# Two transformer blocks on one core: the attention's merge moved by two tiles, output weights placed elsewhere, the expert choice of block 2 cut in three

## The chip, the cores and the metric

The kernel runs on one core of a Trainium2 chip. A core has five engines with instruction queues of their own: TensorE (PE, matmuls and transposes), VectorE (DVE), ScalarE (ACT), GpSimd (POOL) and SyncE (SP, which here only issues DMAs). An engine takes its instructions strictly in order; it waits for others by semaphores. The metric is the device time of one execution in microseconds; lower is better.

## What is computed

1024 tokens of width 1024 go through two blocks in float32. Block 1 has an RG-LRU branch and a multi-head attention branch, which are gated and summed, an output projection, and 32 experts. Block 2 has a hybrid mixer (gated linear attention and pooling), an output projection with layer norm, and 64 experts. The parts that matter here, shortened:

```python
# block 1, 16 heads of 64: chunk-causal attention, then the merge with the other branch
yb = mla(q_c, kv_c, k_pe, ...)          # softmax(q k^T) v, per head
merged = gates[:, :, 0] * ya + gates[:, :, 1] * yb
h = h + merged @ w_out
# block 2
p = multiscale_pool(u, w_pool, pool_scale)
mix = concatenate([o, p], axis=-1)
h = layer_norm(ALPHA * h + mix @ w_out_2, ln1_g, ln1_b)
# expert choice: 4 of 8 groups by the sum of their two best, then 8 of the experts left
scores = sigmoid(h @ w_router); sel = scores + router_bias
gidx  = top_k(top_k(sel by groups of 8, 2).sum(-1), 4)
eidx  = top_k(sel where the group is chosen, 8)
wts   = scores[eidx] / sum * 2.5
```

## The kernel before

Matmuls that need float32 accuracy are made of three float32r matmuls: each operand is split into a high part (ACT, a copy that rounds) and a low part (DVE, the operand minus the high part); `split` (L247, L253), `split_ps` (L259 to L263) and `mm3` (L271 to L273) do this.

**Attention** (`attention`, L834). Heads run one after the other; a head has eight key tiles `kt` of 128. For each tile PE makes the scores `st` (L947 to L949), ACT their exponential `raw` (L950), and three tiles later PE multiplies by the values (L958). `st` has three PSUM buffers, so a scores matmul waits when ACT is three exponentials behind. Beside the tiles, `beside(h, kt)` puts the work for the next head into `fill`: transposes of q and k in tiles 0 and 1 (PE L901, ACT L259 and L262, DVE L260 and L263), row maxima in tiles 3 to 6 (PE L916 into `tm`, three PSUM buffers, DVE L919 and L921), the last reduction `row_piece` after tile 7 (DVE L925, then PE L929). After tile 6 and in tile 2 of the next head `finish` copies the head's output to `y` (ACT L971) and sends its row sums off (SP L973); in tile 4 of the next head `rec` inverts them (DVE L980), writes them to memory (SP L981) and reads them back spread over partitions into the tile `rec` (SP L984), of which there is one.

Heads 2p and 2p+1 are merged as pair p, in six parts of `merge`: part 0 (POOL L992) in the even head 2p+2; parts 1 to 5 in the odd head 2p+3: part 1 (DVE L992) and part 2 (DVE L994) in tile 0, part 3 (DVE L996) in tile 1, part 4 (ACT L999, the high part `mgh`, two of 128x512) and part 5 (DVE L1002, the low part `mgl`, two of 128x512). Part 5 ends with `gates(pr + 1)`: two loads of 512 KB on SP (L1013) for the next pair. `MERGE` (L832) names for each part the first head and the tile. Head 15 has no next head and fewer pieces.

**Mixer of block 2** (`mixer2`, L2048). Its tiles come from pools; `hc` (`c1`, bufs 1, with `v`), `hw` (`wp`, weights, bufs 2), `hs` (`slot()`, ten of 128x1024) are opened in this order and lie so in memory. At its end (L2333 on) the pool weights `wpl` are loaded and split, `v` is transposed back (PE L2353, L263 on DVE writes `mxl`), and four `pool(g)` run.

**Output projection of block 2** (`mixer_out2`, L2366). It loads the output weights in eight pieces of 512 KB (SP L2388) into three tiles `s0`, `s1`, `s2`, and splits each (ACT L247 `woh`, DVE L253 `wol`). These tiles lie over places that the mixer used, so a load waits until the last reader of what lay there is done. Then ten rounds t: for t below 8, 96 matmuls in two halves with DVE L2461 after each, then `norm(t)`: DVE L2407 to L2410, ACT L291 (square root), DVE L292 to L2412, ACT L2414, DVE L2415 (times g), POOL L2416 (plus b; on DVE for t = 7). In round t the half 0 ends with `trans(t-2)` (PE L2428, ACT L2429), the half 1 with `router(t-2)` (PE L2435, ACT L2436 `lg`, ACT L2438 `ah`). After `router(3)` stands the whole expert choice of tokens 0 to 511, `route2` (L2466), a generator with seven pieces of DVE work; its first needs a Tanh on ACT (L2475), which changes ACT's function table, and the next square root changes it back.

Of the kernel before, what the change touches and what calls it, by code (L numbers as in the profile page):

```python
# [7 lines left out]
F32 = mybir.dt.float32  # L8
F32R = mybir.dt.float32r
# [222 lines left out]
class Body:  # L232
# [596 lines left out]
            while posts:  # L829
                step()  # L830

    MERGE = (2, 0), (3, 0), (3, 0), (3, 1), (3, 1), (3, 2)  # L832

    def attention(self, rb, rk, ml):  # L834

# [2 lines left out]
        nc, tc, IN = self.nc, self.tc, self.IN  # L838
        with ExitStack() as cx:
# [227 lines left out]
            def beside(h, kt):  # L1067

                n = h + 1
                fill = []  # L1070
                if kt == 0 and h % 2:
                    load(h // 2 + 2)
                if n < 16:
                    if kt < 2:
                        fill += [(t_piece, n, "kq"[kt], half) for half in range(2)]
                    fill += [(m_piece, n, i, a) for i, a in
                             {3: [(7, 0), (7, 512), (6, 0)], 4: [(6, 512), (5, 0), (5, 512)],
                              5: [(4, 0), (4, 512), (3, 0)], 6: [(2, 0), (1, 0), (0, 0)]}.get(kt, ())]
                    if kt == 5:
                        fill.append((v_piece, n))  # L1080
                    if kt == 7:
                        fill += [(lambda: None,), (row_piece, n)]
                if kt == (3 if h == 15 else 4) and h > 0:
                    fill.append((rec, h - 1))
                if h == 15 and kt == 6:
                    fill.append((merge, 7, 0, 0, 2, nc.vector))
                for part, (late, at) in enumerate(self.MERGE):
                    if h >= late and (h - late) % 2 == 0 and kt == at:
                        fill.append((merge, (h - late) // 2, part, 0, 2, nc.vector if part else nc.gpsimd))
                return fill  # L1090

            self.wo, self.W = {}, {}
# [955 lines left out]
    def mixer2(self, u2):  # L2048

        nc, tc, IN = self.nc, self.tc, self.IN  # L2050
        win = IN["w_in_2"][0]
        with ExitStack() as cx:
            c1 = cx.enter_context(tc.tile_pool(reuse_waits="tile", name="hc", bufs=1))
            wp = cx.enter_context(tc.tile_pool(reuse_waits="tile", name="hw", bufs=2))
            sp = cx.enter_context(tc.tile_pool(reuse_waits="tile", name="hs", bufs=10))
            ep = cx.enter_context(tc.tile_pool(reuse_waits="tile", name="he", bufs=1))
            up = u2.enter_context(tc.tile_pool(reuse_waits="tile", name="u2", bufs=1, side="right"))
# [273 lines left out]
            self.mgh = mix.tile([128, 8, S], F32R, name="mxh")  # L2331
            self.mgl = mix.tile([128, 8, S], F32R, name="mxl")
            with tc.tile_pool(reuse_waits="tile", name="hq", bufs=2, space=PSUM) as pp, tc.tile_pool(reuse_waits="tile", name="hqt", bufs=4, space=PSUM) as pt:  # L2333
                wpl = wp.tile([128, 4, 128], F32, name="w")
                nc.sync.dma_start(wpl, IN["w_pool_2"][0].rearrange("g c d -> c g d"))
                wplh = wp.tile([128, 4, 128], F32R, name="wh")
                wpll = wp.tile([128, 4, 128], F32R, name="wl")
                self.split(wpl, wplh, wpll)
                hg = c1.tile([128, 4], F32, name="hg")
                nc.vector.tensor_scalar(hg, self.v("hg_norm_g_2", 0, 4), 0.5, None, op0=OP.mult)  # L2340

                def pool(g):
                    ph, pl = PH[g]
                    ps = pp.tile([128, S], F32, name="mm")
                    for n in range(2):
                        sl = slice(n * 512, n * 512 + 512)
                        self.mm3(ps[:, sl], [(wplh[:, g], wpll[:, g], ph[:, sl], pl[:, sl])])
                    self.split_ps(ps, self.mgh[:, 4 + g], self.mgl[:, 4 + g], self.v("pool_scale_2", g))

                def back(half, k):  # L2350
                    ps = pt.tile([128, 512], F32, name="tp")
                    for i in range(4):
                        nc.tensor.transpose(ps[:, i * 128:i * 128 + 128], v[:, half * 4 + i, k * 128:k * 128 + 128],  # L2353
                                            self.ident)
                    sl = slice(half * 512, half * 512 + 512)
                    self.split_ps(ps, self.mgh[:, k, sl], self.mgl[:, k, sl], hg[:, k:k + 1])

                for half in range(2):
                    for k in range(4):
                        back(half, k)  # L2360
                        if k % 2:
                            pool(half * 2 + k // 2)
# [3 lines left out]
    def mixer_out2(self, mo):  # L2366
# [5 lines left out]
        with ExitStack() as cx:  # L2372
# [58 lines left out]
            def router(t):  # L2431
# [5 lines left out]
                ah = ep.tile([128, D], F32, name="ah", bufs=1)  # L2437
                nc.scalar.activation(self.plain(ah), self.turned(xf), AF.Copy, scale=self.ALPHA)  # L2438
                (nc.gpsimd if t > 4 else nc.sync).dma_start(self.acc_d[t * 128:t * 128 + 128], ah)
                if t == 3:  # L2440
                    for _ in self.route2(rtp, lg[0], bias, 0, 4):
                        pass
            self.route_late = lambda rp: self.route2(rp, lg[1], bias, 4, 8)
            self.pre2 = {}

# [2 lines left out]
            for t in range(10):  # L2448
# [4 lines left out]
                for half in range(2):  # L2453
                    if t < 8:
# [4 lines left out]
                                     [(self.mgh[:, k, ts_], self.mgl[:, k, ts_], h[:, k], lo[:, k]) for k in range(8)])  # L2459
                        hs = X[t][:, half * 512:half * 512 + 512]  # L2460
                        nc.vector.scalar_tensor_tensor(hs, hs, self.ALPHA, ps, op0=OP.mult, op1=OP.add)  # L2461
                    if t > 1:
                        (router if half else trans)(t - 2)
                if t < 8:
                    norm(t)
                    loadx(t + 2)  # L2466


    def route2(self, rp, lg, bias, t0, t1):
# [286 lines left out]
```

## Time and profile before

| | us |
|---|---|
| median of 3 runs (3194.46, 3202.43, 3207.52) | 3202.43 |
| profiled execution, its own time | 3195.43 |
| its span, first to last instruction | 3193.6 |
| PE busy | 2953.0 (92%) |
| DVE busy | 1814.7 (57%) |
| ACT busy | 1249.6 (39%) |
| POOL busy | 642.9 (20%) |
| granted PE clock, mean share of full speed | 0.961 |

The page's shares are means over the whole span. Which engine holds up a stage is read from that stage's own windows and from the idle time that the timeline shows in brackets ahead of an instruction, with the instruction that ended it. A granted clock of 1.00 is 2.4 GHz, 0.50 is 1.2 GHz.

### The profile page before, as it was taken

The numbers are of one execution on the slowest core, as the hardware profiler recorded it, in microseconds if no ns is written. First come the engines' busy times: TensorE is split into PE (matmuls) and PEld (weight loads), VectorE is DVE, ScalarE is ACT, GpSimd is POOL, SyncE is SP. The second block draws the span as 40 slices with busy tenths as digits, with TensorE's granted clock in tenths as the row PEclk, the third lists the DMA queues.
The fourth block names the chain that finished last, engine by engine and source line by source line (L and its number), as shares of the span: only waits on it lengthen the run. The fifth ranks groups of instructions, "written<-read, shape, count | busy, mean of one in ns | idle before, by whom it ended". The sixth has DMA issues, their size and how long they took to land. (4 is left out here: it accounts for less than half of the span.)

```text
span 3193.6 us, 41876 instructions
## 1 busy us (share of the span) xinstructions
PE 2953.0 (92%) x15865; PEld 2183.8 (68%) x15865; DVE 1814.7 (57%) x2909; ACT 1249.6 (39%) x1929; POOL 642.9 (20%) x495
## 2 busy tenths in 40 slices
PE   5999999998999996999889998978999999999995
PEld 4778778896666893655479787955666666666663
DVE  5545651666666656566446565445655555555556
ACT  3332332444445323444343324332344444444343
POOL 0000000121000103233212232112233232333320
PEclk9999999998999997999989999979999999999997
DMA  3212120244332267999720102337899999999994
GB/s 115 66 53 86 66 73 23 97 163 110 93 93 90 92 219 275 300 330 351 239 104 28 40 18 90 132 137 242 267 282 322 303 327 313 316 316 323 314 307 144
DMA packets 225885, 579.71 MB, mean 182 GB/s; under 512 B 22421, under 2 KB 104005, under 8 KB 225653
## 3 DMA queue, kind: packets, MB, share of 16 engines
q1 hardware_dynamic: 187952, 444.37, 39.6%
q0 software_dynamic: 37296, 132.55, 16.6%
q8 instruction: 127, 2.08, 0.3%
q14 instruction: 78, 0.64, 0.1%
q10 hardware_dynamic: 432, 0.06, 0.0%
HBM read 470.22 MB, written 106.64 MB: 181 GB/s over the span
## 5 line engine op out<-in xcount | busy, mean ns | idle before, releaser
L271 PE MATMUL mm<-uh,wh 128*128 128x512 f32 x640 | 252.6, 395 | 10.8 <-ACT t L505 8.8
L273 PE MATMUL mm<-uh,wl 128*128 128x512 f32 x640 | 251.8, 393 | 0.0
L272 PE MATMUL mm<-ul,wh 128*128 128x512 f32 x640 | 251.7, 393 | 0.0
L1475 PE MATMUL gups<-raw,x 128*128 128x512 f32 (+1 forms) x536 | 236.4, 592 | 0.0
L1622 ACT ACTIVATE th<-gups 128x128 f32<-128x128 f32 (+2 forms) x136 | 49.0, 361 | 418.9 <-PE gups L1475 251.0
L1691 POOL DMA_INDIRECT acc_d<-y,si x68 | 118.3, 1740 | 438.9 <-DMA acc_d<-y,si 145.9
L1623 DVE SCALAR_TENSOR_TENSOR hh<-th,gups 128x128 f32<-128x128 f32 (+2 forms) x136 | 53.1, 390 | 241.9 <-ACT th L1622 235.7
L253 DVE TENSOR_TENSOR gl<-raw,gh 128x1024 fp32r<-128x1024 f32 x142 | 168.1, 1221 | 28.4 <-ACT gh L247 28.3
L1688 DVE TENSOR_SCALAR y<-yps,wsl 128x512 f32<-128x512 f32 (+1 forms) x95 | 71.2, 750 | 196.7 <-ACT y L1686 193.8
L271 PE MATMUL gups<-gh,xh 128*128 128x512 f32 (+1 forms) x440 | 179.8, 409 | 0.9 <-ACT xh L1589 0.9
L1686 ACT ACTIVATE y<-yps,wsl 128x512 f32<-128x512 f32 (+1 forms) x100 | 68.7, 687 | 276.9 <-PE yps L1475 146.9
L273 PE MATMUL gups<-gh,xl 128*128 128x512 f32 (+1 forms) x440 | 176.4, 401 | 0.0
L272 PE MATMUL gups<-gl,xh 128*128 128x512 f32 (+1 forms) x440 | 176.1, 400 | 0.0
L1475 PEld LDWEIGHTS gups<-raw,x 128*128 128x128 f32 (+1 forms) x536 | 95.3, 183 | 116.4 <-issue 116.4
L1579 PEld LDWEIGHTS tp<-ident,xg 128*128 128x128 f32 (+2 forms) x1088 | 114.2, 144 | 74.6 <-issue 38.5
L958 PE MATMUL o<-raw,v 128*128 128x512 f32 (+3 forms) x384 | 163.4, 514 | 0.0
L271 PEld LDWEIGHTS mm<-uh,wh 128*128 128x128 f32 x640 | 121.7, 190 | 38.1 <-ACT t L505 10.6
L247 ACT ACTIVATE gh<-raw 128x1024 fp32r<-128x1024 f32 x142 | 142.9, 1054 | 10.5 <-PE gups L273 7.7
L1579 PE MATMUL tp<-ident,xg 128*128 128x128 f32 (+2 forms) x1088 | 128.5, 262 | 15.5 <-DMA xg<-xf_d,gi 7.1
L273 PEld LDWEIGHTS mm<-uh,wl 128*128 128x128 f32 x640 | 121.6, 190 | 25.7
L272 PEld LDWEIGHTS mm<-ul,wh 128*128 128x128 f32 x640 | 121.7, 190 | 25.3
L950 ACT ACTIVATE raw<-st 128x512 f32<-128x512 f32 (+1 forms) x192 | 92.8, 490 | 117.8 <-PE st L949 116.7
(685 smaller groups left out, 7669.0 us busy)
## 6 DMA issues: line engine op xcount, KB each, us to landing
raw<-in_w_down_dram SPq DMA_DIRECT2D x69, 1024.0 KB
raw<-in_w_gate_dram SPq DMA_DIRECT2D x136, 512.0 KB
raw<-in_w_up_dram SPq DMA_DIRECT2D x136, 512.0 KB
w<-in_w_in_dram SPq DMA_DIRECT2D x20, 1024.0 KB
s<-in_w_down_dram SPq DMA_DIRECT2D x17, 1024.0 KB
s<-in_w_gate_dram SPq DMA_DIRECT2D x34, 512.0 KB
s<-in_w_up_dram SPq DMA_DIRECT2D x34, 512.0 KB
b<-in_w_gate_dram SPq DMA_DIRECT2D x22, 512.0 KB
```

What stands on the lines that cost most here:

```text
L247: nc.scalar.activation(hi, src, AF.Copy)
L253: e.tensor_tensor(lo, src, hi.bitcast(F32), op=OP.subtract)
L271: nc.tensor.matmul(out, lh, rh, start=start and i == 0, stop=False, **kw)
L272: nc.tensor.matmul(out, lh, rl, start=False, stop=False, **kw)
L273: nc.tensor.matmul(out, ll, rh, start=False, stop=stop and i == n - 1, **kw)
L950: nc.scalar.activation(raw[:, a - kt * 128:b - kt * 128], st, AF.Exp)
L958: nc.tensor.matmul(O[h][a // 512][:, a % 512:a % 512 + b - a], v, p[:, a - kt * 128:b - kt * 128], start=kt == 0, stop=kt == (7 if a >= 51 ...
L1475: nc.tensor.matmul(out, x, w, start=start and i == 0, stop=stop and i == len(pairs) - 1, **kw)
L1579: nc.tensor.transpose(ps[:, k // 4, (k % 4) * R:(k % 4) * R + R], xg[:R, k * 128:k * 128 + 128], self.ident[:R, :R])
L1686: nc.scalar.activation(y[:R, 0:512], ps[0][:R], AF.Copy, scale=w)
L1688: nc.vector.tensor_scalar(y[:R, 512:1024], ps[1][:R], w, None, op0=OP.mult)
L1691: nc.gpsimd.indirect_dma_start(out=acc_d, out_offset=bass.IndirectOffsetOnAxis(ap=si, axis=0), in_=y[:R], in_offset=None, compute_op=OP.add)
```

## The change

It has three parts. In the attention, parts 4 and 5 of the merge move from tiles 1 and 2 to tiles 3 and 4, and the loop over `MERGE` stands ahead of `rec` in `fill`, so that part 5 reads the tile `rec` before the next pair's `rec` is written. In `mixer2` the pool `hw` is opened ahead of `hc`, and the pool weights and their two parts are taken from `slot()`. In `mixer_out2`, `route2` is no longer run at once after `router(3)`, but by `advance`: three pieces after `norm(5)`, three after `norm(6)`, the last after half 0 of round 7; and `trans(6)` moves from round 8 to just ahead of `norm(7)`.

```diff
-    MERGE = (2, 0), (3, 0), (3, 0), (3, 1), (3, 1), (3, 2)
+    MERGE = (2, 0), (3, 0), (3, 0), (3, 1), (3, 3), (3, 4)
...
+                for part, (late, at) in enumerate(self.MERGE):
+                    if h >= late and (h - late) % 2 == 0 and kt == at:
+                        fill.append((merge, (h - late) // 2, part, 0, 2, nc.vector if part else nc.gpsimd))
                 if kt == (3 if h == 15 else 4) and h > 0:
                     fill.append((rec, h - 1))
                 if h == 15 and kt == 6:
                     fill.append((merge, 7, 0, 0, 2, nc.vector))
-                for part, (late, at) in enumerate(self.MERGE):
-                    if h >= late and (h - late) % 2 == 0 and kt == at:
-                        fill.append((merge, (h - late) // 2, part, 0, 2, nc.vector if part else nc.gpsimd))
...
+            wp = cx.enter_context(tc.tile_pool(reuse_waits="tile", name="hw", bufs=2))
             c1 = cx.enter_context(tc.tile_pool(reuse_waits="tile", name="hc", bufs=1))
-            wp = cx.enter_context(tc.tile_pool(reuse_waits="tile", name="hw", bufs=2))
...
-                wpl = wp.tile([128, 4, 128], F32, name="w")
+                wpl = slot()[:, :512].rearrange("p (g d) -> p g d", g=4)
                 nc.sync.dma_start(wpl, IN["w_pool_2"][0].rearrange("g c d -> c g d"))
-                wplh = wp.tile([128, 4, 128], F32R, name="wh")
-                wpll = wp.tile([128, 4, 128], F32R, name="wl")
+                wplh, wpll = [z[:, a] for z in [slot(F32R).rearrange("p (a g d) -> p a g d", a=2, g=4)] for a in range(2)]
...
-                if t == 3:
-                    for _ in self.route2(rtp, lg[0], bias, 0, 4):
-                        pass
+            first = self.route2(rtp, lg[0], bias, 0, 4)
+
+            def advance(n):
+                for _ in range(n):
+                    next(first, None)
...
-                    if t > 1:
+                    if t > 1 and (half or t != 8):
                         (router if half else trans)(t - 2)
+                    if t == 7 and not half:
+                        advance(1)
+                if t == 7:
+                    trans(6)
                 if t < 8:
                     norm(t)
                     loadx(t + 2)
+                    advance({5: 3, 6: 3}.get(t, 0))
```

ACT in head 3, tiles 1 to 4, before (L950 exponential, L999 high part of the merge, L971 output to `y`):

```order
380 L262 ACTIVATE kq_4615<-tm,gk 96x512 x2
381 L950 ACTIVATE raw<-st 128x512
382 L999 ACTIVATE mgh_4740<-rec 128x512
383 L999 ACTIVATE mgh_4742<-rec 128x512
384 L950 ACTIVATE raw<-st 128x256
385 L950 ACTIVATE raw<-st 128x512
386 L971 ACTIVATE y<-o_5195 128x512
387 L950 ACTIVATE raw<-st 128x128
388 L950 ACTIVATE raw<-st 128x512 x2
```

and after:

```order
380 L262 ACTIVATE kq_4615<-tm,gk 96x512 x2
381 L950 ACTIVATE raw<-st 128x512
382 L950 ACTIVATE raw<-st 128x256
383 L950 ACTIVATE raw<-st 128x512
384 L971 ACTIVATE y<-o_5195 128x512
385 L950 ACTIVATE raw<-st 128x128
386 L950 ACTIVATE raw<-st 128x512
387 L999 ACTIVATE mgh_4740<-rec 128x512
388 L999 ACTIVATE mgh_4742<-rec 128x512
389 L950 ACTIVATE raw<-st 128x512
```

The two L999 stand four exponentials and one L971 later; nothing else changes its place.

DVE in head 3, from the transposes' low parts (L263) to the inversion L980, before (L996 part 3 of the merge, L1002 part 5, L919 and L921 the row maxima):

```order
512 L263 SCALAR_TENSOR_TENSOR kq_4615<-tm,gk,kq_4615 96x512 x2
513 L996 SCALAR_TENSOR_TENSOR rec<-m_4756,rec 128x1024
514 L1002 SCALAR_TENSOR_TENSOR mgl_4741<-rec,mgh_4740 128x512
515 L1002 SCALAR_TENSOR_TENSOR mgl_4743<-rec,mgh_4742 128x512
516 L919 TENSOR_REDUCE nm_4609<-tm 128x1 x2
517 L921 TENSOR_REDUCE nm_4609<-tm 64x1
518 L919 TENSOR_REDUCE nm_4609<-tm 128x1 x2
519 L921 TENSOR_REDUCE nm_4609<-tm 64x1
520 L919 TENSOR_REDUCE nm_4609<-tm 128x1 x2
521 L921 TENSOR_REDUCE nm_4609<-tm 64x1
522 L980 RECIPROCAL r_5265<-r_5265 128x8
```

and after:

```order
512 L263 SCALAR_TENSOR_TENSOR kq_4615<-tm,gk,kq_4615 96x512 x2
513 L996 SCALAR_TENSOR_TENSOR rec<-m_4756,rec 128x1024
514 L919 TENSOR_REDUCE nm_4609<-tm 128x1 x2
515 L921 TENSOR_REDUCE nm_4609<-tm 64x1
516 L919 TENSOR_REDUCE nm_4609<-tm 128x1 x2
517 L921 TENSOR_REDUCE nm_4609<-tm 64x1
518 L919 TENSOR_REDUCE nm_4609<-tm 128x1 x2
519 L921 TENSOR_REDUCE nm_4609<-tm 64x1
520 L1002 SCALAR_TENSOR_TENSOR mgl_4741<-rec,mgh_4740 128x512
521 L1002 SCALAR_TENSOR_TENSOR mgl_4743<-rec,mgh_4742 128x512
522 L980 RECIPROCAL r_5265<-r_5265 128x8
```

The two L1002 stand behind the six rows of tiles 3 and 4, still ahead of L980.

ACT in the output projection of block 2, from `router(3)` on, before (L2438 is `ah`, L2475 the Tanh of `route2` with its table, L291 and L2414 of `norm`, L2429 `trans`, L2436 `router`):

```order
1094 L2438 ACTIVATE ah<-xf 128x8x128
1095 L2475 ACT_TABLE_LOAD
1096 L2475 ACTIVATE sc<-lg_14872 128x256
1097 L291 ACT_TABLE_LOAD
1098 L291 ACTIVATE rsa_t<-bvar 128x1
1099 L2414 ACTIVATE xf<-xr,bnb,brs 128x1024
1100 L2429 ACTIVATE xT<-tp 128x512 x2
1101 L2436 ACTIVATE lg_14873<-tp 128x64
1102 L2438 ACTIVATE ah<-xf 128x8x128
```

and after (`route2` stands eight lines further down in the new file, so L2483 is L2475 of before):

```order
1100 L2438 ACTIVATE ah<-xf 128x8x128
1101 L291 ACTIVATE rsa_t<-bvar 128x1
1102 L2414 ACTIVATE xf<-xr,bnb,brs 128x1024
1103 L2483 ACT_TABLE_LOAD
1104 L2483 ACTIVATE sc<-lg_14871 128x256
1105 L2429 ACTIVATE xT<-tp 128x512 x2
1106 L2436 ACTIVATE lg_14872<-tp 128x64
1107 L2438 ACTIVATE ah<-xf 128x8x128
1108 L291 ACT_TABLE_LOAD
1109 L291 ACTIVATE rsa_t<-bvar 128x1
1110 L2414 ACTIVATE xf<-xr,bnb,brs 128x1024
```

L291 and L2414 of `norm(5)` now stand ahead of the table load and the Tanh, and `trans(4)` and `router(4)` ahead of the table load that L291 of `norm(6)` needs. On DVE the norm's instructions move in the same way: `norm(5)` ahead of pieces 1 to 3, `norm(6)` ahead of pieces 4 to 6, one L2461 ahead of piece 7.

## Rows read from the trace of the kernel before

**Rows 1.** Windows, odd heads 3 to 13: start:end us, length, engines' busy us, clock, DMA share.

```profile
805.63:828.92 23.29, 20.73 (x98) 14.59 (x97) 16.32 (x33) 11.06 (x23) 0.00 (x0) 0.93 0.50 146
...
sum 140.48, PE 125.05 PEld 89.22 DVE 97.94 ACT 66.78 POOL 0.00; mean PE 20.84 PEld 14.87 DVE 16.32 ACT 11.13 POOL 0.00
```

**Rows 2.** Windows, the even heads 4 to 14, same columns: sum and means of six.

```profile
sum 113.21, PE 113.21 PEld 84.00 DVE 70.85 ACT 61.68 POOL 14.10; mean PE 18.87 PEld 14.00 DVE 11.81 ACT 10.28 POOL 2.35
```

**Rows 3.** Timeline of ACT, head 3: start us, us, line, operation [idle before <-releaser].

```profile
816.70 1.15 ACT L999 ACTIVATE mgh<-rec 128x512 fp32r<-128x512 f32 x2 [2.29 <-DVE rec L996]
```

**Rows 4.** Timeline of DVE, head 3, columns as in Rows 3.

```profile
817.37 1.29 DVE L1002 SCALAR_TENSOR_TENSOR mgl<-rec,mgh 128x512 fp32r<-128x512 f32 x2 [0.70 <-ACT mgh L999]
```

**Rows 5.** Timeline of DVE, second half of head 4.

```profile
842.73 0.49 DVE L919 TENSOR_REDUCE nm<-tm 128x1 f32<-128x320 f32 x1 [1.03 <-PE tm L916]
...
845.35 0.82 DVE L919 TENSOR_REDUCE nm<-tm 128x1 f32<-128x512 f32 x2 [0.42 <-PE tm L916]
...
849.38 0.20 DVE L925 TENSOR_REDUCE mz<-nm 128x8 bf16<-128x24 f32 x1
```

**Rows 6.** Timeline of PE, end of head 4.

```profile
849.84 0.61 PE L929 MATMUL tm<-identb,mz 128*97 128x128 bf16 x8
```

**Rows 7.** Timeline of SP, head 3.

```profile
827.93 0.46 SPq L984 DMA_DIRECT2D rec<-rec_d  x1
```

**Rows 8.** Timeline of POOL, head 4.

```profile
831.65 2.35 POOL L992 TENSOR_TENSOR rec<-rec,y 64x1024 f32<-64x1024 f32 x1 [40.44 <-DMA rec<-rec_d]
```

**Rows 9.** Timeline of PE, start of the output projection of block 2.

```profile
1973.08 0.54 PE L271 MATMUL mm<-woh,mxh 128*128 128x256 f32 x1 [3.31 <-DVE mxl L263]
1974.34 0.58 PE L272 MATMUL mm<-wol,mxh 128*128 128x256 f32 x1 [0.72 <-DVE wol L253]
```

**Rows 10.** Timeline of SP there: the eight loads of output weights.

```profile
1968.51 13.89 SPq L2388 DMA_DIRECT2D s<-in_w_out_dram  x8
```

**Rows 11.** Windows around there, columns as in Rows 1.

```profile
1958.50:1968.50 10.00, 8.32 (x53) 6.78 (x51) 8.44 (x12) 8.43 (x12) 0.00 (x0) 1.00 0.01 2
1973.08:1990.05 16.97, 12.20 (x51) 11.03 (x51) 8.16 (x7) 6.77 (x7) 0.65 (x2) 0.60 1.07 356
1990.25:1996.00 5.75, 5.75 (x49) 5.75 (x49) 2.17 (x4) 1.72 (x2) 0.00 (x0) 1.00 0.14 54
```

**Rows 12.** Timeline of DVE, output projection, token tiles 5 to 7.

```profile
2067.68 0.29 DVE L2476 TENSOR_SCALAR sc<-sc 128x256 f32<-128x256 f32 x1 [5.15 <-ACT sc L2475]
...
2072.75 0.29 DVE L2493 TENSOR_TENSOR goh<-e_r,gi8f 128x128 f32<-128x128 f32 x1
...
2078.02 0.42 DVE L2512 TENSOR_TENSOR W<-W,ws 128x256 f32<-128x256 f32 x1
...
2080.27 1.28 DVE L2407 BATCH_NORM_STATS2 bst<-xr 128x6 f32<-128x512 f32 x2
...
2087.71 1.29 DVE L2461 SCALAR_TENSOR_TENSOR xr<-xr,mm 128x512 f32<-128x512 f32 x2
...
2113.01 2.06 DVE L2416 TENSOR_TENSOR xf<-xf,b 128x1024 f32<-128x1024 f32 x1
```

**Rows 13.** Timeline of ACT there.

```profile
2063.70 2.22 ACT L2438 ACTIVATE ah<-xf 128x1024 f32<-128x1024 f32 x1
...
2082.01 0.20 ACT L291 ACTIVATE rsa_t<-bvar 128x1 f32<-128x1 f32 x1 [13.06 <-DVE bvar L2410]
```

**Rows 14.** Timeline of POOL there.

```profile
2087.94 2.87 POOL L2416 TENSOR_TENSOR xf<-xf,b 128x1024 f32<-128x1024 f32 x1 [27.08 <-DVE xf L2415]
```

**Rows 15.** Windows there, columns as in Rows 1.

```profile
2075.85:2086.17 10.32, 0.00 (x1) 0.00 (x1) 7.08 (x24) 2.96 (x4) 0.00 (x0) 0.65 0.00 1
2086.17:2092.60 6.43, 6.43 (x30) 6.43 (x31) 4.75 (x10) 2.67 (x4) 2.87 (x1) 0.50 0.16 62
```

**Rows 16.** One line's instructions: duration ns min/median/max.

```profile
L2141 DVE TENSOR_TENSOR kt<-slot,E x28: 672/680/2376, 1662.5 to 1903.4; 128x512 f32<-128x512 f32 x28
```

**Rows 17.** Windows, expert stage of block 2, columns as in Rows 1.

```profile
2400.00:2800.00 400.00, 398.93 (x2291) 247.38 (x2288) 229.53 (x318) 170.25 (x256) 120.29 (x85) 1.00 0.99 314
```

## The prediction

> **What bounds the kernel now.** PE is busy nearly the whole span, so a change pays only where PE waits or runs at the lower clock. I read the windows by stage first, then the timelines around the stretches where PE stands. Three such stretches touch the change.
>
> In the attention a head lies between the copies of two successive heads' first halves. The six even heads 4 to 14 take 113.21 us, all of it PE work, 18.87 each [rows 2]. The six odd heads 3 to 13, with the same matmuls, take 140.48 us, of which PE is busy 125.05 [rows 1]. The difference of 27.3 us has two parts: 15.4 us of idle PE, 2.57 a head, and 11.8 us in which the same matmuls ran longer; the granted clock is 0.93 in such a head and 1.00 in the even ones, so part of a head after the stop ran at 1.2 GHz. What stops PE is ACT: the high part L999 stands 2.29 us and waits for DVE's L996 [rows 3], and the exponentials behind it, which would free the score buffers, wait too. In the order ahead the two L999 stand before four exponentials and a copy that are ready.
>
> At the start of block 2's output projection the eight weight loads are issued from 1968.51 on [rows 10]; in the ten microseconds before, the DMA engines are 0.01 busy [rows 11]. PE's first matmul there waits 3.31 us for DVE's last low part of the mixer [rows 9]; from it to 1990.05 PE is busy 12.20 of 16.97 us at a clock of 0.60 [rows 11], because the loads dribble in while DMA is full at 1.07.
>
> In the expert choice DVE works on route2 from 2067.68 and reaches norm(5) only at 2080.27 [rows 12]; PE stands 10.32 us and then runs 6.43 us at 0.50 [rows 15].
>
> **Merge, two tiles later.** Nothing is added; two ACT and two DVE instructions per odd head and two SP loads move. Behind four exponentials L999 finds L996 done, so the 2.29 us stop goes, and with it PE's idle time and, since the lower clock is seen in these heads alone, the slow matmuls. What is late next is DVE. It does 16.32 us in an odd head and 11.81 in an even one [rows 1, 2], 4.5 more. All but L1002's 1.29 us [rows 4] of it, 3.2, stands ahead of the row maxima, among the low parts of q and k; an even head has waits for PE there and another of 1.03 us behind [rows 5]. I take this part as covered, since DVE's waits in an even head make 18.87 - 11.81 = 7 us. L1002 now stands behind the sixth row, where an even head has only 0.42 and 0.22 us of waiting left before L925 [rows 5]: L925 comes 1.29 - 0.64 = 0.65 us late. It ends at 849.58 in an even head and PE reads it at 849.84 [rows 5, 6], 0.26 of slack, so PE stands 0.39 us. An odd head becomes 18.87 + 0.39 = 19.26, six of them 115.6, a gain of **24.9 us**. Bounds: no lag and a little more from head 15, 28; L1002's full 1.29 plus half of the other 3.2 showing up, 2.9 a head, 10. I take the near end since the waits that cover it are rows of an even head, where the PE work is the same.
>
> The two loads L1013 move on SP behind the send of the row sums and ahead of L981 and L984, which bring back the next pair's sums; L984 also waits for L1002 now. L984 is issued at 827.93 [rows 7], POOL's L992 takes its result at 831.65 [rows 8], and DVE reads L992's product only in the next odd head, a whole head of 18.9 us later. One MB at the 146 GB/s of such a head [rows 1] is 7 us; it fits. Cost nothing; without that cover it would be 7 us a head.
>
> **Pool order in the mixer.** With the weight pool lowest, the three staging tiles of the output weights no longer lie over the values v, read until the mixer's end, but over weight tiles whose last readers are the last projection matmuls. The first load then follows on SP only the pool weights' load and the loads behind it wait for the last projection chunk, some ten microseconds earlier than now. Four MB at 356 GB/s [rows 11] take 11.8 us, in the empty ten microseconds, so all but the last two pieces (their tile is used twice) are there when the mixer ends.
>
> The added wait: the pool weights' tile is now one of the ten slots, and its high part on ACT stands until DVE has split the slot's last tenant. In ACT's order that is right ahead of the back transposes' copies; I put it at 0.8 us from the order alone, between 0 and one DVE split of 1.2. Then PE starts steadily not at 1974.34 [rows 9] but at 1975.15. The work from 1973.08 to 1996.00, counted at the full clock, is half of 12.20 plus 5.75, 11.85 us [rows 11]. A restart after a stop ran 6.43 us at half clock [rows 15]: it does 3.2 of this, the other 8.65 at full, so the tile ends at 1975.15 + 15.05 = 1990.2 in place of 1996.0. Gain **5.8 us**; were the whole stretch at half clock, 1975.15 + 6.1 x 2 + 5.75 = 1993.1 and 2.9; were it all at full clock, 9.
>
> **Expert choice in three pieces.** DVE's order is then norm(5), pieces 1 to 3, two L2461, norm(6), pieces 4 to 6, L2461, piece 7, L2461, norm(7). ACT ends ah(3) at 2065.92 [rows 13] and takes the square root of norm(5). From that instruction to POOL's L2416 it is 2082.01 to 2087.94, 5.93 us [rows 13, 14]: POOL runs from 2071.85 to 2074.7 (2.87).
>
> Here a row adds a price. L2141, which has both inputs in SBUF, takes 0.68 us, and up to 2.38 [rows 16]: the long ones overlap an addition on POOL and end a whole duration after it. Piece 1's second instruction and piece 4's have two such inputs and now stand beside POOL's L2416; each waits for its end. The Trainium skill, "SBUF — State Buffer", section "SBUF: two separate sides", calls the port pair that DVE and GpSimd share an exclusive lock held for a whole instruction, for a DVE operation with two SBUF inputs; it speaks against placing pieces beside L2416, and this trace shows it for L2141. If it did not hold for the pieces, the sum below would end about 4 us earlier.
>
> So pieces 1 to 3 end at 2074.7 + 4.7 = 2079.4 (4.7: 2067.68 to 2072.75 less the first instruction) [rows 12]; two L2461, 1.29; norm(6) begins at 2080.7, its square root 1.74 later (2080.27 to 2082.01), at 2082.4, L2416 from 2088.4 to 2091.2. Pieces 4 to 6 last 2072.75 to 2078.02, 5.3: 2096.5. L2461 and piece 7, 0.7 and 2.3: 2099.5; L2461, 0.7; norm(7)'s square root at 2101.9, L2416, on DVE and 2.06 long, ends at 2101.9 + 5.93 + 2.06 = 2109.9. It ends at 2115.07 now [rows 12], and trans(7), router(7) and the experts follow it. Gain **5.2 us**; without the lock 9; a lock at each of the pieces' two-input operations, 3. The 10.32 us hole goes, but a new one of some ten opens ahead of trans(7): DVE becomes the bound there, not PE.
>
> **Sum.** 24.9 + 5.8 + 5.2 = 35.9 us. The profiled execution took 3195.43, 7.0 below the median of 3202.43: 3159.5 there, **3166** in the median. Behind these stages PE is busy 398.93 of 400 us in the expert stage while DMA is at 0.99 [rows 17], so a gain ahead of it is kept as long as the loads start earlier too; they wait for buffers that PE frees.
>
> **Rivals.**
> (a) DVE binds the odd heads. For: its 16.32 us no longer overlap a stop of PE, and it works in small steps with PE. If half of the 7 us that it waits in an even head stay waits, an odd head takes 16.3 + 3.5 = 19.8, near my forecast; if all 7 stay, 23.3, and the merge gains nothing: 3191. I weigh a loss of half the gain: 3178.
> (b) DMA, full at 0.99 in the experts, hands back what the last two parts gain, 11: 3177. Against: no wait for weights shows in PE's 1.07 us of idle there.
> (c) The output weights come no earlier, held on SP behind the pool weights' load, whose slot waits for DVE: minus 5.8, and 0.8 lost: 3173.
> (d) Slower: L984, behind 1 MB and L1002, brings the row sums so late that POOL's L992 holds DVE's L992, and it ACT and PE, in each odd head. The cover is 18.9 us. It decides past that: to lose all 36 us and 16 more, L984 must land 27 us late in six heads. The loads' 7 us say no.
> (e) The lock does not hold: 3162, inside the range.
>
> **Chances.** Forecast with (e) 0.68, (a) 0.12, (b) 0.08, (c) 0.09, (d) 0.03. The range goes down to 3152 (28 + 9 + 9 of the bounds give 3156, and the runs of before lie up to 8 us from their median) and up to 3182 (any of (a) to (c), or two of them in part). Half a percent, 16 us, is about what a measurement of this kernel can tell from no change: faster 0.90, same 0.07, slower 0.03.
>
> **What would show it.** Odd heads of 19.3 us with a clock of 1.00, no idle before L999, and a wait of PE's L929 for L925 of some 0.4. The first output-weight load issued near 1956, and one stop of PE there, not three. The first norm after router(3) right behind ah(3); a DVE operation of piece 1 that lasts 2 to 3 us; PE idle ahead of trans(7) by about ten. I am wrong if the odd heads keep the clock of 0.9 (then something else stops PE in tile 3 or 4), if the DVE waits of rows 5 are not there in an odd head, or if the experts' stage grows by what came before it.

## The result and the profile after

The changed kernel takes 3160.2 us (median of four runs, 3158.24 to 3160.81) against 3201.6 for the kernel before on the same chip: a ratio of 0.987, interval 0.985 to 0.989, or 41 us. Forecast were 3166 and a range from 3152 to 3182. The profiled execution took 3159.88 us, its span is 3157.8; the forecast for it was 3159.5.

The page of the kernel after, its first lines (span; busy time, share, instructions):

```profile
span 3157.8 us, 41871 instructions
...
PE 2938.1 (93%) x15865; PEld 2173.7 (69%) x15865; DVE 1816.9 (58%) x2909; ACT 1249.1 (40%) x1929; POOL 636.7 (20%) x495
```

PE was busy 2953.0 us before, with the same 15865 matmuls: of the 36 us between the two spans 15 are matmuls that ran shorter (the mean granted clock is 0.965 and was 0.961), and 21 are idle time of PE.

**Attention.** Windows of the kernel after, each from the copy L971 of one even head's first half to that of the next even head, that is an odd and an even head together, the first and the sum of six; columns as in rows 1:

```profile
804.79:842.94 38.15, 37.88 (x194) 27.90 (x193) 27.95 (x60) 21.40 (x44) 2.36 (x1) 1.00 0.33 98
...
sum 228.80, PE 227.18 PEld 167.40 DVE 167.70 ACT 128.49 POOL 14.19; mean PE 37.86 PEld 27.90 DVE 27.95 ACT 21.41 POOL 2.37
```

The same twelve heads took 140.48 + 113.21 = 253.69 us before [rows 1, 2]: 24.9 us less, and the clock is 1.00 throughout. The waits of PE (engine, line, waited for; us in total, times, longest), all of them in the six odd heads of the kernel before, then all in the twelve heads of the kernel after, and ACT's timeline at the merge in head 3, which answers to rows 3:

```profile
PE st L947 <- ACT raw L950: 15.4, 6, 2.6
```

```profile
PE tm L929 <- DVE mz L925: 1.6, 6, 0.3
```

```profile
815.50 0.60 ACT L950 ACTIVATE raw<-st 128x512 f32<-128x512 f32 x1 [0.23 <-PE st L949]
816.00 1.14 ACT L999 ACTIVATE mgh<-rec 128x512 fp32r<-128x512 f32 x2
```

L999 no longer waits; what is left is the wait for the last row maximum, 0.27 us in each odd head.

**Start of the output projection.** SP, ACT and PE there (rows 9 and 10 of before), then windows (rows 11), the first from the mixer's first `pool(g)`, the others of the first token tile:

```profile
1934.46 22.46 SPq L2388 DMA_DIRECT2D s<-in_w_out_dram  x8
```

```profile
1939.72 0.63 ACT L247 ACTIVATE slot<-slot 128x512 fp32r<-128x512 f32 x1 [1.29 <-DVE slot L253]
```

```profile
1940.40 0.50 PE L271 MATMUL mm<-slot 128*128 128x512 f32 x1 [2.46 <-ACT slot L247]
1952.87 0.39 PE L271 MATMUL mm<-woh,mxh 128*128 128x256 f32 x1 [2.15 <-ACT woh L247]
1954.89 0.48 PE L272 MATMUL mm<-wol,mxh 128*128 128x256 f32 x1 [1.63 <-DVE wol L253]
```

```profile
1940.40:1942.81 2.41, 2.41 (x7) 1.48 (x8) 1.60 (x4) 1.26 (x2) 0.00 (x0) 0.70 1.07 367
1952.87:1958.53 5.66, 4.03 (x19) 3.83 (x20) 5.66 (x6) 4.68 (x5) 0.00 (x0) 0.70 0.42 133
1958.53:1968.00 9.47, 9.47 (x82) 9.47 (x81) 5.05 (x6) 3.41 (x3) 0.00 (x0) 1.00 0.50 185
```

The loads are issued 2.4 us ahead of the mixer's first back transpose (at 1936.90) and no longer 10 us behind it; the price is ACT's 1.29 us for the slot, and behind it PE's stop of 2.46 us ahead of the first `pool(g)`, whose matmuls then start at the lower clock (0.70 in that window). Ahead of the first tile PE stops twice, where one stop was forecast, and runs through the tile then. From the mixer's first back transpose to the end of that tile PE idles 3.5 us less and its matmuls take 2.9 us less.

**Expert choice.** DVE and POOL in rounds 5 and 6, and the new hole of PE ahead of trans(7) as a window:

```profile
2043.62 0.28 DVE L2484 TENSOR_SCALAR sc<-sc 128x256 f32<-128x256 f32 x1
2043.93 3.18 DVE L2485 TENSOR_TENSOR sel<-sc,rbias 128x256 f32<-128x256 f32 x1
...
2060.23 0.28 DVE L2501 TENSOR_TENSOR goh<-e_r,gi8f 128x128 f32<-128x128 f32 x1
2060.55 0.29 DVE L2503 TENSOR_REDUCE gm<-goh 128x32 f32<-128x128 f32 x1
2060.87 2.52 DVE L2504 TENSOR_SCALAR gm<-gm 128x32 f32<-128x32 f32 x1
```

```profile
2043.83 3.01 POOL L2416 TENSOR_TENSOR xf<-xf,b 128x1024 f32<-128x1024 f32 x1 [11.04 <-DVE xf L2415]
2060.45 2.90 POOL L2416 TENSOR_TENSOR xf<-xf,b 128x1024 f32<-128x1024 f32 x1 [13.62 <-issue]
```

```profile
2068.64:2080.89 12.25, 0.00 (x1) 0.03 (x1) 9.04 (x19) 4.47 (x4) 0.00 (x0) 0.50 0.00 2
```

Two DVE operations last until POOL's addition is over: 2043.83 + 3.01 = 2046.84 and 2060.45 + 2.90 = 2063.35, where they end at 2047.11 and 2063.39. The hole of 10.32 us [rows 15] is gone, and one of 12.25 stands ahead of trans(7). Seen from PE, less idle time is the smaller part of this gain. From the end of token tile 0 to the last `lg`, before and after, as windows:

```profile
1995.85:2121.44 125.59, 109.23 (x866) 108.23 (x865) 60.68 (x180) 46.60 (x49) 23.14 (x11) 0.90 0.35 122
```

```profile
1967.98:2086.44 118.46, 104.47 (x866) 103.78 (x865) 65.48 (x180) 46.94 (x50) 23.04 (x11) 0.92 0.36 129
```

PE's idle time falls from 16.4 to 14.0 us, and its busy time, with the same 866 matmuls, by 4.8 us: before there were two holes, of 10.32 and 5.29 us, with slow matmuls behind each, and now there is one.

The three stretches gain 24.7, 6.4 and 7.1 us. Between the first two of them 4.0 us are lost in this execution (870.3 us from the last high part of the merge to the mixer's first back transpose, 866.3 before), of which more below; 1.6 us are gained ahead of the attention and behind the choice.

### The profile page after: what moved, and what is told of

The parts are those of the page before. It is cut to its first block, busy times and chain, and to the rows that moved or that the text cites. A ratio compares the mean times of both kernels' runs of the same rounds, so it can differ in the third digit from the quotient of the medians.

```text
span 3157.8 us, 41871 instructions
## 1 busy us (share of the span) xinstructions
PE 2938.1 (93%) x15865; PEld 2173.7 (69%) x15865; DVE 1816.9 (58%) x2909; ACT 1249.1 (40%) x1929; POOL 636.7 (20%) x495
## 5 line engine op out<-in xcount | busy, mean ns | idle before, releaser
L271 PE MATMUL mm<-uh,wh 128*128 128x512 f32 x640 | 253.0, 395 | 10.8 <-ACT t L505 8.8
L271 PE MATMUL gups<-gh,xh 128*128 128x512 f32 (+1 forms) x440 | 180.1, 409 | 0.9 <-ACT xh L1589 0.9
L958 PE MATMUL o<-raw,v 128*128 128x512 f32 (+3 forms) x384 | 156.4, 495 | 0.0
L271 PEld LDWEIGHTS mm<-uh,wh 128*128 128x128 f32 x640 | 121.5, 190 | 37.9 <-ACT t L505 10.6
L950 ACT ACTIVATE raw<-st 128x512 f32<-128x512 f32 (+1 forms) x192 | 93.1, 491 | 102.9 <-PE st L949 101.8
```

The costliest lines, as they stand in the source:

```text
L271: nc.tensor.matmul(out, lh, rh, start=start and i == 0, stop=False, **kw)
L950: nc.scalar.activation(raw[:, a - kt * 128:b - kt * 128], st, AF.Exp)
L958: nc.tensor.matmul(O[h][a // 512][:, a % 512:a % 512 + b - a], v, p[:, a - kt * 128:b - kt * 128], start=kt == 0, stop=kt == (7 if a >= 51 ...
```

## The experiments

Three stretches are compared in all kernels, from the starts of instructions in each trace, in us: A from the first copy L971 to the last high part L999 of the merge (attention); B from the mixer's first back transpose (L2353) to the second L2461 of token tile 0, its end (start of the projection; the line is L2464 in the kernels with the third part); C from there to the last `lg` (L2436, the choice).

| kernel | A | B | C | median | ratio to before (interval) |
|---|---|---|---|---|---|
| before | 324.2 | 37.5 | 125.6 | 3201.6 | |
| after | 299.5 | 31.1 | 118.4 | 3160.2 | 0.9871 (0.9850 to 0.9891) |
| e1_merge | 299.5 | 39.6 | 126.1 | 3168.7 | 0.9900 (0.9881 to 0.9919) |
| e2_places | 326.0 | 31.1 | 125.3 | 3192.8 | 0.9973 (0.9962 to 0.9985) |
| e3_choice | 325.9 | 37.5 | 118.3 | 3192.3 | 0.9977 (0.9966 to 0.9989) |
| e10_after_again | 299.6 | 31.1 | 118.5 | 3156.8 | 0.9862 (0.9840 to 0.9884) |
| e4_rest_late | 299.5 | 31.1 | 112.0 | 3154.1 | 0.9858 (0.9834 to 0.9882) |
| e5_add_dve | 299.5 | 30.5 | 117.7 | 3153.4, one run | |
| e6_low_at_3 | 301.9 | 30.6 | 118.3 | 3161.4, one run | |
| e7_pool_w_ep | 299.4 | 30.1 | 118.5 | 3157.2, one run | |
| e8_one_tile | 311.0 | 32.0 | 118.6 | 3172.4, one run | |
| e12_low_fixed | 296.8 | 31.1 | 118.5 | 3159.6 | 0.9881 (0.9853 to 0.9908) |
| e9_all | 302.1 | 29.4 | 112.0 | 3151.4 | 0.9849 (0.9830 to 0.9868) |
| e11_all_fixed | 297.0 | 29.4 | 112.0 | 3145.8 | 0.9834 (0.9809 to 0.9858) |

### Each part alone

The merge alone, on the kernel before:

```diff
-    MERGE = (2, 0), (3, 0), (3, 0), (3, 1), (3, 1), (3, 2)
+    MERGE = (2, 0), (3, 0), (3, 0), (3, 1), (3, 3), (3, 4)
```

with the loop over `MERGE` ahead of `rec`.

> The first part alone, on the kernel before: parts 4 and 5 of the merge two tiles later. My theory: the three parts add up, and this one is worth what the attention shows in the trace after, 24.7 us: about 3177 in the median (ratio 0.992), odd and even heads together 38.1 us in place of 42.2. Rival (the expert stages, where DMA is nearly full, hand gains back): less than 20 us, with the loss inside the expert stages.

A falls by 24.7 us, as in the kernel after, and the median by 29.9, more than expected. The gain does not vanish in the expert stages. (B is 2.1 us longer than before here, though nothing is changed in that stretch.)

The places alone: the weight pool first, the pool weights in slots, the rest as before.

> The second part alone: the weight pool lowest and the pool weights in slots. My theory: 6.4 us from the mixer's end to the end of the first token tile, as in the trace after, with the added ACT wait of about 1.3 us in it; the 3 us that the kernel after loses between the first expert stage and the mixer are of the clock or the moment, not of this part: about 3195. Rival: those 3 us come from this part (the first loads of the mixer wait for other tenants of the memory), then only about 3 us are gained and the trace shows the loss there.

B falls by 6.4 us. The slow matmuls that the trace after has at the start of the mixer's projection are not there, so they are not of this part: the 49 matmuls take 11.46 us at a clock of 1.00, as in the kernel before. They come and go between runs of the same kernel. Here they are in the trace of the kernel after, and in the same kernel once more (e10_after_again):

```profile
1595.13:1608.85 13.72, 13.72 (x49) 11.01 (x50) 3.49 (x3) 2.23 (x3) 0.00 (x0) 0.82 0.26 78
```

```profile
1596.11:1607.57 11.46, 11.46 (x49) 9.34 (x50) 3.34 (x3) 1.71 (x2) 0.00 (x0) 1.00 0.29 93
```

That is 2.3 of the 3.3 us by which these two executions differ between A and B (870.3 and 867.0). The rest was not traced to a cause; over all fourteen traces the stretch takes 864.4 to 870.6 us, 868.4 with the places alone.

The choice alone: `route2` in pieces and `trans(6)` moved, the rest as before.

> The third part alone: the expert choice in three pieces. My theory: DVE becomes the bound of that stage, 7 us gained, about 3195, with two DVE operations of 2.5 to 3.2 us beside POOL's addition and a PE hole of about 12 us ahead of the last transposes. Rival: in the kernel after part of these 7 us came from the earlier output weights; then 5 us or less here.

C falls by 7.3 us, and the median by 6.3; the two long DVE operations last 3.17 and 2.52 us here too. The earlier output weights have no share in it.

> The kernel after, unchanged, once more, on the same chip as the four edits together and with more runs. My theory: 38 us below the kernel before, the sum of the three parts alone in their traces (24.9, 6.4 and 7.1), ratio 0.988. Rival: the parts take from each other, 33 us or less.

43 us, ratio 0.986, where 38 were expected. The three parts alone give 24.7 + 6.4 + 7.3 = 38.4 us in the stretches and 29.9 + 5.8 + 6.3 = 42.0 in the medians: they add up. That the medians show some 4 us more than the stretches is left open. In the trace of before one of six odd heads takes 21.61 us and others up to 24.57, so what the merge's wait costs may differ between executions as it does between heads; no run here measures that apart.

### One tile later is not enough

```diff
-    MERGE = (2, 0), (3, 0), (3, 0), (3, 1), (3, 3), (3, 4)
+    MERGE = (2, 0), (3, 0), (3, 0), (3, 1), (3, 2), (3, 3)
```

> The kernel after, with parts 4 and 5 of the merge only one tile later than before (tiles 2 and 3). My theory: L999 stands behind just one more exponential, ACT still stops there for about 2 us until DVE's L996, and PE stands about 2 us in every odd head as before, with the lower clock behind it: a pair of heads 40 to 42 us in place of 38.1. Rival: one more score tile in hand is enough for PE, and a pair takes 38.1 as with two tiles.

Windows of pairs of heads, the first and the sum, then PE's waits in them:

```profile
806.23:845.39 39.16, 37.91 (x194) 27.90 (x193) 27.94 (x60) 21.33 (x45) 2.37 (x1) 1.00 0.32 95
...
sum 234.98, PE 227.49 PEld 167.41 DVE 167.63 ACT 127.97 POOL 14.15; mean PE 37.91 PEld 27.90 DVE 27.94 ACT 21.33 POOL 2.36
```

```profile
PE o L958 <- ACT y L971: 7.5, 6, 1.3
```

ACT still waits, 2.01 us in each odd head, as expected. But PE stops 1.25 us only, and the clock stays at 1.00 in all six pairs: a pair takes 39.2 us, between the 40 to 42 of the theory and the 38.1 of the rival. The exponential that now stands ahead of L999 was worth 1.3 us of PE's stop, which ends with the copy L971 here and no longer with an exponential; with the shorter stop the slow matmuls went as well. (A is 11.5 us longer; 6.2 of it are the six pairs, 5 the last head, below.)

### The low parts one tile earlier, and the queue of SP

```diff
-    MERGE = (2, 0), (3, 0), (3, 0), (3, 1), (3, 3), (3, 4)
+    MERGE = (2, 0), (3, 0), (3, 0), (3, 1), (3, 3), (3, 3)
```

> The kernel after, with part 5 of the merge one tile earlier (tile 3, behind its three rows). My theory: DVE's 1.3 us then fall where DVE still has 0.6 us of waiting, L925 comes early enough, and PE's wait of 0.27 us for it goes: a pair of heads 37.85 in place of 38.1, six of them 1.6 us. Rival: DVE waits there for ACT's L999, the rows of tile 4 come late and PE waits for their buffers: 38.2 or more.

The pairs of heads:

```profile
sum 226.08, PE 226.08 PEld 167.92 DVE 167.13 ACT 128.49 POOL 14.22; mean PE 37.68 PEld 27.99 DVE 27.86 ACT 21.41 POOL 2.37
```

PE waits for nothing in them, and they take 2.7 us less, more than the 1.6 expected. Yet A is 2.4 us longer, since head 15 loses 5.1. SP and DVE of that head:

```profile
1042.20 0.54 SPq L1013 DMA_DIRECT2D g<-g_d  x1
1042.79 0.42 SPq L1013 DMA_DIRECT2D m<-m_d  x1
1043.76 0.32 SPq L981 DMA_DIRECT2D rec_d<-r  x1
1050.00 0.46 SPq L984 DMA_DIRECT2D rec<-rec_d  x1
```

```profile
1056.24 1.22 DVE L992 TENSOR_TENSOR rec<-rec,y 64x1024 f32<-64x1024 f32 x1 [7.25 <-DMA rec<-rec_d]
```

In head 15 `rec` stands in tile 3, so part 5 in tile 3 comes ahead of it and its two loads of 512 KB (L1013) stand ahead of L981 and L984. From L981 to L984 it is 6.2 us (3.7 in the kernel after, where the loads come behind), DVE's L992 starts at 1056.24 in place of 1051.67, and PE stops 6.0 us for the merge. L981 itself goes out no later (1043.76, in the kernel after 1044.19), so the delay does not come from DVE, which makes the sums. To undo that alone:

```diff
-                    if h >= late and (h - late) % 2 == 0 and kt == at:
+                    if h >= late and (h - late) % 2 == 0 and kt == at + (h == 15 and part == 5):
```

> The kernel after with part 5 of the merge in tile 3, but in tile 4 in head 15. My theory: the six pairs of heads stay at 37.7 us without a wait of PE, and the end of the attention is no longer 5 us late: 2.8 us less than the kernel after from head 2 to the last high part. Rival: as above.

PE's waits at the end of the attention with part 5 in tile 3 (e6_low_at_3), then with the fix:

```profile
PE mm L271 <- ACT mgh L999: 6.0, 1, 6.0
```

```profile
PE mm L271 <- ACT mgh L999: 0.9, 1, 0.9
```

Part 5 and its loads move together here; that the loads are the cause rests on the rows of SP above. A is 296.8, 2.7 us below the kernel after, as expected; the medians (3159.6 and 3156.8 to 3160.2) do not tell it apart.

### What lengthens the two DVE operations

```diff
-                (nc.vector if t == 7 else nc.gpsimd).tensor_tensor(self.turned(xf), self.turned(xf), self.plain(b),
+                (nc.vector if t in (5, 6, 7) else nc.gpsimd).tensor_tensor(self.turned(xf), self.turned(xf), self.plain(b),
```

> The kernel after, with the addition of norm(5) and norm(6) (L2416) on DVE in place of POOL, so that nothing runs on POOL beside the pieces. My theory, that the two DVE operations of 3.18 and 2.52 us waited for POOL's addition: the same two instructions last 0.43 and about 0.18, and though DVE takes on 2 x 2.1 us of additions, norm(7) comes no later than in the kernel after (by 0 to 1 us earlier). Rival, that their length has another cause (the operands, the pieces' memory): they stay long, and norm(7) is about 4 us later.

The same two instructions:

```profile
2041.15 0.42 DVE L2485 TENSOR_TENSOR sel<-sc,rbias 128x256 f32<-128x256 f32 x1
...
2057.47 0.29 DVE L2504 TENSOR_SCALAR gm<-gm 128x32 f32<-128x32 f32 x1
```

They last 0.42 and 0.29 us with nothing on POOL, and C is 0.7 us shorter though DVE does two additions more: the waits cost DVE more than the work that POOL took from it.

### The last pieces behind norm(7)

```diff
-                    advance({5: 3, 6: 3}.get(t, 0))
+                    advance({5: 3, 7: 4}.get(t, 0))
```

and the single piece after half 0 of round 7 left out.

> The kernel after, with the expert choice's pieces 4 to 7 behind norm(7) in place of behind norm(6) and after half 0 of round 7. My theory says that DVE's chain through these pieces holds norm(7): without them ahead of it the root of norm(7) waits only for ACT, about 2066.7 in place of 2073.0 in the trace after, and everything behind is 6.3 us earlier: about 3154. The pieces fit into DVE's 10.5 us of idle behind norm(7). Rival: PE or ACT holds norm(7) nearly as late (2 us or less gained), or the pieces hold up the second half's choice and nothing is gained.

C falls by 6.4 us, so DVE's pieces held norm(7), and the median is the expected 3154, with an interval that overlaps that of the kernel after. But in the profiled execution (span 3155.4 against 3157.8) 2.4 of the 6.4 us are given back behind the last `lg`: from there to the end it is 1073.8 us, 1071.4 in the kernel after. PE's waits there, with a DVE operation and its neighbour on POOL:

```profile
PE tp L2428 <- DVE xf L2416: 6.1, 1, 6.1
PE cnt L2533 <- DVE ex L2511: 4.9, 1, 4.9
```

```profile
2086.45 2.39 DVE L2482 TENSOR_SCALAR xg<-xg 128x256 f32<-128x256 f32 x1 [2.92 <-ACT xg L2481]
2086.78 1.91 POOL L2540 COPY cols<-tilep 128x1536 bf16<-128x1536 bf16 x1
```

The second wait is new: PE waits for the choice of the other 512 tokens, on DVE. 2.1 us of that choice's delay are again a DVE operation beside POOL (L2482, 2.39 us in place of 0.29). Why they met here is seen in PE's clock in the 9 us behind the last `lg`, in this kernel and in the kernel after:

```profile
2081.60:2090.60 9.00, 7.57 (x29) 4.54 (x28) 5.84 (x27) 5.66 (x6) 3.30 (x7) 0.91 0.54 177
```

```profile
2086.40:2095.40 9.00, 7.59 (x22) 4.88 (x22) 3.97 (x42) 5.75 (x6) 3.29 (x7) 0.52 0.52 177
```

POOL's work there follows transposes of PE. At the higher clock the copy L2540 starts 5.2 us behind the last `lg`, in the kernel after 6.0, and so it overlaps L2482; the higher clock also brings PE to its wait sooner. In the two kernels below the clock there is 0.52 again, the copy starts at 6.0 us, L2482 lasts 0.29 us and the wait is not there. So this loss goes with the clock of the execution; that one of the other edits took it away is not shown.

### The pool weights' place

```diff
-                wpl = slot()[:, :512].rearrange("p (g d) -> p g d", g=4)
+                wpl = ep.tile([128, S], F32, name="qt0")[:, :512].rearrange("p (g d) -> p g d", g=4)
```

and `kt0` for the two parts.

> The kernel after, with the pool weights and their two parts in the places of the qt0 and kt0 tiles (dead by then) in place of two slots. My theory: the stop of ACT ahead of the split of the pool weights is the wait for the slot's last tenant, 1.29 us; it goes, the output projection begins about 1.2 us earlier against the last projection of the mixer, and nothing else changes. Rival: the stop comes from the load itself, and stays.

ACT's split follows the one ahead of it without a stop:

```profile
1934.20 1.05 ACT L247 ACTIVATE slot<-slot 128x1024 fp32r<-128x1024 f32 x1
1935.15 0.62 ACT L247 ACTIVATE kt<-qt 128x512 fp32r<-128x512 f32 x1
```

The projection's first matmul comes 2.4 us earlier against the mixer, more than the 1.2 expected: the stop ahead of the first `pool(g)` is 1.06 us in place of 2.46, and the slow matmuls behind it are gone too. But B is only 1.0 us shorter: behind its steady start PE runs 7.41 us at 0.60, where the kernel after ran 3.64 us at 0.53 (1954.89 to 1958.53).

```profile
1949.59:1957.00 7.41, 7.41 (x40) 7.41 (x41) 7.21 (x7) 4.88 (x6) 0.00 (x0) 0.60 0.73 248
```

### All of them together

The four edits (pieces 4 to 7 last, part 5 in tile 3, the pool weights' places, norm(5)'s addition on DVE):

> The kernel after with four edits together: pieces 4 to 7 behind norm(7); part 5 of the merge in tile 3; the pool weights in the places of qt0 and kt0; norm(5)'s addition on DVE. My theory: what their traces showed adds up against the kernel after: 3.0 (behind it PE waits for the second half's choice), 2.8, 1.0 (of 2.4, the rest lost to a longer stretch at the lower clock) and 0.4: about 7 us below the kernel after on the same chip. Rival: DVE, which all of them load later, gives some back: 4 us or less.

5.4 us below the kernel after on the same chip, 7.6 by the spans (3149.2 and 3156.8), where 7 were expected, with head 15's 5 us still in it. The two intervals overlap. With that undone:

> The four edits together, with part 5 in tile 4 again in head 15 alone, so that there the two loads of gates stand behind the read of the inverted sums on SP and not ahead of it. In the trace of part 5 in tile 3 the read came 2 us later and its data 4.6 us later in that head, and PE stood 6.0 us for the merge. My theory: this goes, and the kernel is 5 us below the four edits without it (3151 to 3146, span 3149 to 3144). Rival: the late data came from other transfers, and nothing changes.

3145.8 us, ratio 0.983, span 3143.6: just below what was expected, and the lowest median of the study, 11 to 14 us below the two medians of the kernel after. The intervals of the ratios overlap; of its five runs four (3142.2 to 3149.4) lie below every run of the kernel after (3153.7 to 3160.8), and one, 3154.6, does not.

## Why the prediction was right

**Merge.** Forecast 24.9 us, measured 24.9 in the twelve heads. Each step held: the two L999 find their data, the idle time and the slow matmuls both go, and DVE is next, late at L925. The wait forecast there was 0.39 us, the trace has 0.27, and PE's busy time in a pair is 0.12 us more than two even heads had before (37.86 and 2 x 18.87): that the digits agree is luck. Of the 0.64 us of DVE's waiting that the forecast set against L1002, rows 5 show 0.42; the rest is this row of the same timeline:

```profile
847.52 0.49 DVE L919 TENSOR_REDUCE nm<-tm 128x1 f32<-128x320 f32 x1 [0.22 <-PE tm L916]
```

**Places.** Forecast 5.8, measured 6.4. Two terms were off and offset each other. PE's steady start came 1.2 us later than forecast (1954.89 against 1974.34 + 0.81, the mixer now being 21.45 us earlier): the added ACT wait was taken at 0.8 us and is 1.29, and that PE's matmuls behind it would run at the lower clock was not in the sum. The stretch at the lower clock behind it was taken at 6.43 us, from the choice's restart [rows 15]; it ended 3.64 us after the start (1958.53), which gives back 1.4. Rows 9 were also misread, without harm to the sum. PE's first matmul L271 was said to wait for DVE's last low part of the mixer; in the kernel after it starts at 1952.87, while that low part is still at work, and behind ACT's first split weight, for which it waits:

```profile
1952.43 1.28 DVE L263 SCALAR_TENSOR_TENSOR mxl<-mm,vec,mxh 128x1024 fp32r<-128x1024 f32 x1
```

**Choice.** Forecast 5.2, measured 7.1 in the kernel after. DVE's chain agrees with its working to 0.1 us up to POOL's second addition: on the clock of before, shifted by the 28.07 us that the trace is ahead there, the root of norm(6) starts at 2082.32 (forecast 2082.4) and L2416 at 2088.52 (2088.4). The step that was mis-sized is the one behind: norm(7) ends 6.3 us earlier than before and not 5.2. The sum put all of pieces 4 to 6, 5.3 us, behind POOL's addition; L2501 and L2503 ran before it ended, and from its end to the end of piece 6 it is 4.55 us (2063.35 to 2067.90). Another 0.35 us is that the L2464 begin ahead of the end of what stands before them, and 0.2 us are shorter L2415 and L2416. The rest of the 7.1, 0.8, lies outside this chain. That the sum follows DVE's chain is right; it does not say that 4.8 us of the gain come as shorter matmuls, behind one hole of PE in place of two.

The waits at the shared port were forecast, some 4 us in the sum, and are 2.75 and 2.3 us; the first place was right too. They end 0.27 and 0.04 us after POOL's additions, sooner than the whole duration that was read from L2141. In piece 4 it was not the two-input L2501 that waited, which started just ahead of POOL, but the one-input L2504 two instructions later. The Trainium skill, "SBUF — State Buffer", section "SBUF: two separate sides", names DVE operations in a two-port mode beside those with two inputs and says that whichever starts first holds the pair. The order of L2501, POOL and L2504 in this trace agrees; that L2504 ran in such a mode no run here shows. The reduction L2503 lasted 0.29 us beside POOL's addition and was not held.

**Offset to the median.** The sum was made against the profiled execution and came out 0.4 us off there; the 7 us added for the median were of the runs of before, and the kernel after does not have them (its profiled execution is at its median). Most of the 6 us between forecast and median come from that. The 0.4 us are luck in part: the three stretches gained 38.2 us, 2.3 more than forecast, and the 4.0 us lost between A and B and the 1.6 us gained at both ends, none of which the prediction treats, took about as much back.

**The rivals.** That DVE binds the odd heads (a) did not come true beyond the 0.27 us. That DMA in the experts gives the gain back (b): PE is busy 398.72 us of 400 there as before [rows 17], and each part alone kept its gain. That the loads come no earlier (c): they are issued 34 us earlier, 13 more than the mixer moved. The slower rival (d) was right as a mechanism and rightly priced as covered: in head 15, where the sums are needed in the same head, two loads ahead of L984 cost 5 us; in the other odd heads POOL's L992 and a whole head lie between.

## What to carry to other kernels

An instruction on an in-order engine that waits for another engine stops all that stands behind it; put it where its data are there, and count what the next engine has left in that place, as here 0.6 us of DVE's waits against 1.3 us of work. A part worked into a loop has to be read once more at the loop's ends: the same move that gained 2.7 us in six pairs of heads lost 5.1 in the last head, through a queue on which the others have a whole head of slack. When work is split to fill an engine's gaps, see what runs beside it: here DVE waited twice for an addition on POOL. And count the stops of PE, not only their length, since matmuls behind a stop may run at the lower clock: one hole of 12.25 us in place of two of 10.32 and 5.29 was worth 7 us.

## What the runs showed of the hardware

A stop of PE of 1.25 us left the granted clock at 1.00 in six cases of six (e8_one_tile); a stop of 2.57 us was followed by matmuls at the lower clock in five of six odd heads of the kernel before. The sixth, as a window of the kernel before, columns as in rows 1:

```profile
889.94:911.55 21.61, 19.04 (x98) 13.96 (x97) 16.31 (x33) 11.06 (x23) 0.00 (x0) 1.00 0.55 158
```

The other five took 23.25 to 24.57 us, 1.6 to 3.0 more for the same stop.

A one-input multiplication and addition on DVE over 128x32 values, 0.18 to 0.29 us alone, lasted 2.52 us beside an addition on POOL, and one over 128x256 values, 0.29 us alone, 2.39 us beside a copy on POOL of 1.91 us (e4_rest_late); the reduction just ahead of the first was not held.

A small write and the read (256 KB) that brings it back went behind 1 MB of loads on the same SP queue: the read was issued 6.2 us after the write, 3.7 without the loads ahead, and its reader started 4.6 us later (e6_low_at_3 and the kernel after).
